# Selecting matmuls as 64x32 tiles on two banks, and GpSimd's products moved to VectorE, in an S5 and attention trunk

## The chip, the cores and the metric

The kernel runs on one core of a Trainium2 chip. The metric is the device time of one execution in microseconds (us); the time before is the median of three runs. One execution was also recorded by the hardware profiler. In its views PE is TensorE (matmuls), PEld its weight loads, DVE is VectorE, ACT is ScalarE, POOL is GpSimd, SP is SyncE, which issues the DMAs.

## The reference

The reference is a trunk of two layers on 256 tokens of 2048 channels, all in float32: an S5 state-space layer with a gated linear unit (GLU), a gated MLP with a short convolution, a latent attention layer, and a second such MLP. Each sub-layer is wrapped in two RMS norms.

```
x = x + rms(s5_mixer(rms(x)));   x = x + rms(conv_ffn_0(rms(x)))
x = x + rms(mla_mixer(rms(x)));  x = x + rms(conv_ffn_1(rms(x)))

def rmsnorm(x, g):
    y = x32 * lax.rsqrt(jnp.mean(x32 * x32, axis=-1, keepdims=True) + EPS) * g
def s5_mixer(u, ...):            # 128 groups of 16 channels, 64 complex states each
    x_re = jnp.einsum('blgp,gnp->blgn', ub, bb_re);  x_im = ...
    acc_re, acc_im, hl_re, hl_im = lax.associative_scan(combine, (a_r, a_i, x_re, x_im), axis=1)
    y = einsum(hs_re, c_re) - einsum(hs_im, c_im) + d_skip * ub
    val, gate = jnp.split(gelu(y) @ w_glu + b_glu, 2, axis=-1);  return val * sigmoid(gate)
def conv_ffn(h, ...):
    g = depthwise_conv(h @ w_gate) + conv_b;  return (gelu(g) * (h @ w_up)) @ w_down
```

## The kernel before

Every weight is streamed once from HBM in tiles of 1 MB (`raw`) and split in two parts, so that float32 accuracy comes out of reduced passes: ScalarE writes the high part (`whi`, L73), VectorE the rest (`wlo` = raw - whi, L74; with a gain folded in, L101). Where a weight tile is held back for later use, its parts are called x. Two or three matmuls then make one product (L108 to L110, L114 and L115). The token halves tb = 0, 1 hold 128 rows each.

The S5 layer is the stage from the start to about 262 us. It is computed as 16 blocks (nb = 16), eight groups of channels each. In a loop over the blocks the steps of three neighbouring blocks are written in between each other:

- `part_a`, the frames (L382 to L385) and the powers prepare tables of the recurrence: mostly VectorE (L430 to L435), some ScalarE (bc, L418 to L421).
- `part_k` makes the table K of the block: 128x32 matmuls (L399), one copy by ScalarE (L451) and an addition by VectorE (L452). Then the **selecting matmuls** (L466): their stationary operand is a column range of the constant tile cst that holds ones and zeros, their moving operand is K, so they only pick rows of K and put them elsewhere. There are two banks; into each go 2 x 2 x 4 matmuls: two strips j, an odd and an even part, and four column tiles b of 32 columns. The stationary operand is 128 rows by 32 columns, and in each all but 16 rows are zero. Behind each bank ScalarE copies it into TP (L471).
- `part_e` transposes (L479), `part_v` and `part_r` scan over the states (L495 to L506, matmul L511, then L513, L514), `part_h` makes H (L520), `part_c` the output (L399 with ET, TP, f and H).
- Once a quarter of the output is there, one step of the GLU (24 matmuls of 128x512, L108 to L110; sums L256, L258) stands in each block's place, from block 5 on.

After the S5 blocks `glu_rest` streams the rest of the GLU's weights; bias, sigmoid and product are L627 to L630.

Between the layers the row norms stand in TensorE's way. `finish_chunk` squares a chunk of 512 columns with sums (ScalarE, L139) and multiplies it by the norm's gain (L166): the last of four chunks on VectorE, the others on GpSimd. `rstd1` forms the inverse root: sum tot (L145), the power rs_y on GpSimd (L147), one Newton step on VectorE (L149 to L153). `post_norm` adds to the residual (L172, VectorE), squares, and multiplies by the next norm's gain (L178): the first two chunks on GpSimd, the others on VectorE. `pre_scale` writes the diagonal xh (L182), and the transposing matmuls L191 wait for it; all matmuls of the next layer stand behind these. Meanwhile the first weights of the next layer are split and held; in both FFNs two of these splits (slots 0 and 4 of `HOLD`) run on GpSimd, the others on VectorE.

Each engine works its own queue in order; the order in a queue is set when the kernel is built, by a scheduler that walks the program with buffers and priorities. So an edit in one place can shift the rows of a queue elsewhere.

Of the kernel before, what the change touches and what calls it, by code (L numbers as in the profile page):

```python
# [15 lines left out]
P = 128  # L16
D = 2048
S = 256
# [19 lines left out]
HOLD = ((0, 2), (4, 6), (8, None), (None, None))  # L38

C_ID, C_PS, C_PR, C_BO, C_DM, C_MK, C_CV = 0, 128, 256, 384, 512, 528, 592  # L40
C_SG, C_NSG, C_TPI, C_FR, C_RS, C_HP, C_MH, C_SL, C_END = 624, 625, 626, 627, 628, 629, 630, 638, 894


@with_exitstack
def tile_trunk(ctx: ExitStack, tc: tile.TileContext, a: dict):
# [4 lines left out]
    def T(pl, shape, dt=F32, tag=None, bufs=None):  # L50
        cnt[0] += 1
        kw = {"bufs": bufs} if bufs else {}
        return pl.tile(shape, dt, tag=tag, name=f"{tag}_{cnt[0]}", **kw)
# [11 lines left out]
    def accb():  # L65
        return T(ps, [P, 512], F32, "acc")
# [96 lines left out]
    def finish_chunk(f, fst, tb, n, g):  # L163
        c = f[tb][:, n * 512 : (n + 1) * 512]
        sq_acc(c, fst[tb][:, n : n + 1])
        (dve if n == NCH - 1 else pool).tensor_tensor(c, c, g[0][:, n * 512 : (n + 1) * 512], op=ALU.mult)  # L166

    def post_norm(f, fst, tb, x, xst, g):
        r = rstd1(fst[tb], D)
        for n in range(NCH):  # L170
            c = slice(n * 512, (n + 1) * 512)
            dve.scalar_tensor_tensor(x[tb][:, c], f[tb][:, c], r, x[tb][:, c], op0=ALU.mult, op1=ALU.add)  # L172
            if xst is None:
                sync.dma_start(a["out"][tb * P : (tb + 1) * P, c], x[tb][:, c])
                continue
            sq_acc(x[tb][:, c], xst[:, n : n + 1])
            if g is not None:
                (pool if n < 2 else dve).tensor_tensor(f[tb][:, c], x[tb][:, c], g[0][:, c], op=ALU.mult)  # L178

    def pre_scale(xst):  # L180
        d = T(env["ap"], [P, 512], F32, "xh", 2)[:, :P]
# [79 lines left out]
    def s5(f):  # L261
        with tc.tile_pool(name="s5", bufs=2) as q1:
# [175 lines left out]
            def part_k(sb, e1, ff):  # L438
# [17 lines left out]
                    op=ALU.add,  # L456
                )
                TP = T(q1, [P, 4, NG * P], F32, "TP")
                for jj in range(2):
                    bank = accb()  # L460
                    for j in range(2):
                        for odd in range(2):
                            o = C_SL + (2 * (2 * jj + j) + odd) * 32
                            for b in range(4):
                                r = 16 * (2 * b + odd)
                                pe.matmul(  # L466
                                    bank[32 * b : 32 * b + 32, j * 256 : (j + 1) * 256].rearrange("p (g c) -> p g c", g=NG),
                                    cst[:, o : o + 32], K[:, :, r : r + P],
                                    start=j == 0 and odd == 0, stop=j == 1 and odd == 1, tile_position=(0, 32 * b),
                                )  # L470
                    act.activation(TP[:, 2 * jj : 2 * jj + 2, :], bank.rearrange("p (j c) -> p j c", j=2), AF.Copy)  # L471
                return U, TP

            def part_e(e1):
# [207 lines left out]
    def ffn(l, tail, gains, f, fst, done):  # L682
        with tc.tile_pool(name=f"ff{l}", bufs=2) as q1:
# [42 lines left out]
            for part, npair in enumerate(PARTS):  # L726
                hid = []
                for pr in range(p0, p0 + npair):
                    banks = [wk(), wk()] if pr == 0 else [[wk(), wk()] for _ in range(2)]
                    held = []  # L730
                    for which, w in enumerate((wg, wu)):
                        for kh in range(2):
                            v = w[:, 8 * kh : 8 * kh + 8, pr * S : (pr + 1) * S]
                            if pr == 0:
                                held.append((which, kh, wunit(v, 8, S, slots=HOLD[len(held)], onpool=(0, 4))))
                            else:
                                inner(banks[which], kh, wunit(v, 8, S))
                    if held:
# [345 lines left out]
def _constants():  # L1084
# [20 lines left out]
    for j in range(4):  # L1105
        for odd in range(2):
            q = np.arange(16)
            c[32 * j + 16 + q, C_SL + (2 * j + odd) * 32 + 16 * odd + q] = 1.0
    return c


# [65 lines left out]
```

## Time and profile before

| what | us |
|---|---|
| median of three runs | 2207.73 (2205.02 to 2211.3) |
| the profiled execution's own time | 2209.45 |
| span of its profile | 2207.7 |
| S5, from the first select to the last block's work | 36.57 to 262 |
| busy in the span: TensorE, VectorE, ScalarE, GpSimd | 2109.7, 1415.1, 1125.0, 75.7 |
| waits of TensorE for xh at the three layer edges | 7.92, 8.42, 8.37 |
| selecting matmuls, busy in all | 60.3 |

A row of a group or timeline gives the start, the duration, the engine, the line and operation, output<-inputs, tile, shape and count; in square brackets stands how long the engine had been idle before, and what ended that. A float32 matmul appears as two passes where it is not split by hand, so a select block of 32 matmuls is 64 records.

### The profile page before, as it was taken

To read this page: it belongs to the slowest core of one execution; us is meant where nothing else is said; L and a number is where in the kernel's file an instruction comes from. 1 tells how busy PE (TensorE), PEld (TensorE's weight loads), DVE (VectorE), ACT (ScalarE), POOL (GpSimd) and SP (SyncE) were. 2 spreads that over 40 slices of the span, in tenths; PEclk is the share of its full clock that TensorE was granted. 3 is DMA by queue.
4 is the path that set the end of the run, shared out by engine and by line. 5 is a ranking of instruction groups with operands and counts; after the bars stand their busy time and mean duration, and the time that the engine had idled before them with its cause. 6 is when DMAs were issued, how large, how long until landed. Compare 5 with 4: busy or idle time off the path is not lost. (4 is left out here: it accounts for less than half of the span.)

```text
span 2207.7 us, 32426 instructions
## 1 busy us (share of the span) xinstructions
PE 2109.7 (96%) x13268; PEld 1779.4 (81%) x13268; DVE 1415.1 (64%) x1904; ACT 1125.0 (51%) x1695; POOL 75.7 (3%) x93
## 2 busy tenths in 40 slices
PE   3899999899999999999989999989999999999997
PEld 2666777888888888888878898788888888888886
DVE  7999675766456656655676665566646655665566
ACT  6676444455455435544464555545545544554444
POOL 0000010200000000000010000120000000000001
PEclk9999999999999999999999999999999999999999
DMA  4132376455555555556563434635555556555554
GB/s 129 47 100 75 103 246 208 148 191 189 183 195 184 190 191 190 186 178 201 185 200 121 145 122 137 212 128 179 186 191 191 191 178 203 189 188 181 197 184 149
DMA packets 280965, 374.80 MB, mean 170 GB/s; under 512 B 9200, under 2 KB 196208, under 8 KB 279792
## 3 DMA queue, kind: packets, MB, share of 16 engines
q1 hardware_dynamic: 280816, 372.73, 51.5%
q8 instruction: 104, 1.70, 0.3%
q14 instruction: 45, 0.37, 0.1%
HBM read 370.61 MB, written 2.10 MB: 169 GB/s over the span
## 5 line engine op out<-in xcount | busy, mean ns | idle before, releaser
L74 DVE TENSOR_TENSOR wlo<-raw,whi 128x1024 fp32r<-128x1024 f32 (+2 forms) x640 | 763.3, 1194 | 595.7 <-ACT whi L73 592.6
L73 ACT ACTIVATE whi<-raw 128x1024 fp32r<-128x1024 f32 (+2 forms) x640 | 658.3, 1031 | 646.8 <-PE wk L114 249.2
L114 PE MATMUL wk<-act,whi 128*128 128x512 f32 x2688 | 944.8, 396 | 0.0
L115 PE MATMUL wk<-act,wlo 128*128 128x256 f32 x2688 | 754.4, 281 | 0.0
L114 PEld LDWEIGHTS wk<-act,whi 128*128 128x128 f32 x2688 | 504.4, 188 | 121.1
L115 PEld LDWEIGHTS wk<-act,wlo 128*128 128x128 f32 x2688 | 507.8, 189 | 0.3
L109 PE MATMUL acc<-wlo,hh 128*128 128x512 f32 x652 | 255.8, 392 | 0.5
L108 PE MATMUL acc<-whi,hh 128*128 128x512 f32 x652 | 255.6, 392 | 0.0
L110 PE MATMUL acc<-whi,hl 128*128 128x512 f32 x652 | 254.3, 392 | 0.0
L109 PEld LDWEIGHTS acc<-wlo,hh 128*128 128x128 f32 x652 | 122.5, 188 | 28.4 <-DVE wlo L74 2.2
L108 PEld LDWEIGHTS acc<-whi,hh 128*128 128x128 f32 x652 | 122.5, 188 | 27.4 <-ACT hh L73 0.5
L110 PEld LDWEIGHTS acc<-whi,hl 128*128 128x128 f32 x652 | 122.5, 188 | 26.9
L108 PE MATMUL acc<-whi,act 128*128 128x512 f32 (+1 forms) x332 | 126.4, 381 | 0.9 <-ACT act L73 0.7
L109 PE MATMUL acc<-wlo,act 128*128 128x512 f32 (+1 forms) x332 | 124.8, 377 | 2.3 <-DVE wlo L74 2.3
L110 PE MATMUL acc<-whi,act 128*128 128x512 f32 (+1 forms) x332 | 124.2, 375 | 0.0
L166 POOL TENSOR_TENSOR f<-f,gb 128x512 f32<-128x512 f32 x24 | 37.3, 1555 | 1866.7 <-issue 1583.9
L763 DVE SCALAR_TENSOR_TENSOR cv<-gs,cw,cv 128x255 f32<-128x255 f32 (+1 forms) x168 | 77.2, 480 | 3.0
L109 PEld LDWEIGHTS acc<-wlo,act 128*128 128x128 f32 x332 | 62.5, 188 | 15.3 <-DVE wlo L74 4.4
L108 PEld LDWEIGHTS acc<-whi,act 128*128 128x128 f32 x332 | 62.5, 188 | 12.7 <-ACT act L73 1.0
L110 PEld LDWEIGHTS acc<-whi,act 128*128 128x128 f32 x332 | 62.5, 188 | 11.4 <-DVE act L74 0.4
L761 ACT ACTIVATE cv<-gs,cb,cw 128x256 f32<-128x256 f32 x84 | 50.5, 601 | 36.5 <-DVE gs L713 36.5
L466 PE MATMUL acc<-K,cst 128*32 128x256 f32 x1024 | 60.3, 388 | 5.0 <-DVE K L452 4.7
(285 smaller groups left out, 2409.3 us busy)
## 6 DMA issues: line engine op xcount, KB each, us to landing
raw<-in_w_gate SPq DMA_DIRECT2D x88, 1024.0 KB, 4.9
raw<-in_w_up SPq DMA_DIRECT2D x88, 1024.0 KB, 4.9
raw<-in_w_down SPq DMA_DIRECT2D x88, 1024.0 KB, 4.9
raw<-in_w_glu SPq DMA_DIRECT2D x32, 1024.0 KB, 6.1
raw<-in_w_o SPq DMA_DIRECT2D x16, 1024.0 KB, 5.0
raw<-in_w_ukv SPq DMA_DIRECT2D x8, 1024.0 KB, 5.4
gb<-in_norm_g SPq DMA_DIRECT2D x6, 1024.0 KB, 8.4
raw<-in_w_uq SPq DMA_DIRECT2D x8, 768.0 KB, 4.6
```

Of the source, the lines that this page charges most:

```text
L73: act.activation(hi, src, AF.Copy)
L74: (eng or dve).tensor_tensor(lo, src, hi.bitcast(F32), op=ALU.subtract)
L108: pe.matmul(o, lh, rh, start=first, stop=False)
L109: pe.matmul(o, lh, rl, start=False, stop=False)
L110: pe.matmul(o, ll, rh, start=False, stop=last)
L114: pe.matmul(ov, lh, r, start=first, stop=False)
L115: pe.matmul(ov[:, 0, :], ll, r[:, 0, :], start=False, stop=last)
L166: (dve if n == NCH - 1 else pool).tensor_tensor(c, c, g[0][:, n * 512 : (n + 1) * 512], op=ALU.mult)
L466: pe.matmul(bank[32 * b : 32 * b + 32, j * 256 : (j + 1) * 256].rearrange("p (g c) -> p g c", g=NG), cst[:, o : o + 32], K[:, :, r : r + P ...
L761: act.activation(cv[:, ft, :], gv[:, ft, :], AF.Identity, scale=cw[:, 2, n : n + 1], bias=cb[:, n : n + 1])
L763: dve.scalar_tensor_tensor(cv[:, ft, sh:], gv[:, ft, : S - sh], cw[:, 2 - sh, n : n + 1], cv[:, ft, sh:], op0=ALU.mult, op1=ALU.add,)
```

## The change

Two things change. First, the selecting matmuls: the stationary operand is now 64 rows by 32 columns. Row half jj = 0 reads rows 0 to 63 of K and writes bank 0, row half jj = 1 reads rows 64 to 127 and writes bank 1. Both banks are taken at the start, the innermost loop alternates between them, and the two copies into TP come behind all 32 matmuls. The constant tile becomes 128 columns narrower, since both halves use the same columns. Second, GpSimd gives up its share of the products L166 and L178 and of the weight splits L74; they go to VectorE. It keeps the powers (L147) and small memsets: 98 rows of its queue become 62, and VectorE's 1906 become 1942.

```diff
-C_SG, C_NSG, ..., C_SL, C_END = 624, 625, ..., 638, 894
+C_SG, C_NSG, ..., C_SL, C_END = 624, 625, ..., 638, 766
...
     def finish_chunk(f, fst, tb, n, g):
-        (dve if n == NCH - 1 else pool).tensor_tensor(c, c, g[0][:, n * 512 : (n + 1) * 512], op=ALU.mult)
+        dve.tensor_tensor(c, c, g[0][:, n * 512 : (n + 1) * 512], op=ALU.mult)
...
     def post_norm(f, fst, tb, x, xst, g):
-                (pool if n < 2 else dve).tensor_tensor(f[tb][:, c], x[tb][:, c], g[0][:, c], op=ALU.mult)
+                dve.tensor_tensor(f[tb][:, c], x[tb][:, c], g[0][:, c], op=ALU.mult)
...
+                banks = [accb() for _ in range(2)]
+                for j in range(2):
+                    for odd in range(2):
+                        for b in range(4):
+                            r = 16 * (2 * b + odd)
+                            for jj in range(2):
+                                o = C_SL + (2 * j + odd) * 32
+                                hp = slice(64 * jj, 64 * jj + 64)
+                                pe.matmul(
+                                    banks[jj][32 * b : 32 * b + 32, j * 256 : (j + 1) * 256].rearrange("p (g c) -> p g c", g=NG),
+                                    cst[hp, o : o + 32], K[hp, :, r : r + P],
+                                    start=j == 0 and odd == 0, stop=j == 1 and odd == 1, tile_position=(64 * jj, 32 * b),
+                                )
                 for jj in range(2):
-                    bank = accb()
-                    for j in range(2):
-                        for odd in range(2):
-                            o = C_SL + (2 * (2 * jj + j) + odd) * 32
-                            for b in range(4):
-                                r = 16 * (2 * b + odd)
-                                pe.matmul(
-                                    bank[32 * b : 32 * b + 32, j * 256 : (j + 1) * 256].rearrange("p (g c) -> p g c", g=NG),
-                                    cst[:, o : o + 32], K[:, :, r : r + P],
-                                    start=j == 0 and odd == 0, stop=j == 1 and odd == 1, tile_position=(0, 32 * b),
-                                )
-                    act.activation(TP[:, 2 * jj : 2 * jj + 2, :], bank.rearrange("p (j c) -> p j c", j=2), AF.Copy)
+                    act.activation(TP[:, 2 * jj : 2 * jj + 2, :], banks[jj].rearrange("p (j c) -> p j c", j=2), AF.Copy)
...
-                                held.append((which, kh, wunit(v, 8, S, slots=HOLD[len(held)], onpool=(0, 4))))
+                                held.append((which, kh, wunit(v, 8, S, slots=HOLD[len(held)])))
...
-            c[32 * j + 16 + q, C_SL + (2 * j + odd) * 32 + 16 * odd + q] = 1.0
+            c[32 * j + 16 + q, C_SL + (2 * (j % 2) + odd) * 32 + 16 * odd + q] = 1.0
```

Lines behind the select move by two in the changed kernel (L466 to L467, L471 to L473, L479 to L481, L495 to L497, L511 to L513); lines ahead of it keep their numbers. In the rows that follow, a number behind a name tells one use of a buffer from another.

TensorE's queue around the select of one early block, before:

```order
L479 MATMUL wk_450<-cst_73,e_86_350 128x128 x4
L479 MATMUL wk_456<-cst_73,e_86_350 128x128 x4
L466 MATMUL acc_413<-K_44_179,cst_73 32x256 x16
L466 MATMUL acc_431<-K_44_179,cst_73 32x256 x16
L511 MATMUL wk_462<-R_386,cst_73 128x256
```

And in the changed kernel (acc_413 and acc_414 are the two banks; the alternation goes on for 32 rows):

```order
L481 MATMUL wk_450<-cst_73,e_86_350 128x128 x4
L481 MATMUL wk_456<-cst_73,e_86_350 128x128 x2
L467 MATMUL acc_413<-K_44_179,cst_73 32x256
L467 MATMUL acc_414<-K_44_179,cst_73 32x256
...
L481 MATMUL wk_456<-cst_73,e_86_350 128x128 x2
L513 MATMUL wk_462<-R_386,cst_73 128x256
```

The two banks were filled one behind the other and are now filled in turns; two of the eight transposes of `part_e` moved behind the select here. From block 5 on the order of the other matmuls is as before.

VectorE's queue between FFN 0 and the attention, from the sum tot of the norm to the diagonal xh, before (x and raw are the attention's first weights, gkv the gain folded into them):

```order
L145 TENSOR_REDUCE tot_10186<-st_781_4240 128x1
L101 SCALAR_TENSOR_TENSOR x_1737_10374<-raw_10367,gkv_76,x_1737_10374 128x512
L149 TENSOR_SCALAR rs_m_1694_10190<-tot_10186 128x1
L101 SCALAR_TENSOR_TENSOR x_1737_10374<-raw_10367,gkv_76,x_1737_10374 128x512
L151 SCALAR_TENSOR_TENSOR rs_u_1695_10192<-rs_m_1694_10190,rs_y_1693_10188 128x1
L101 SCALAR_TENSOR_TENSOR x_1739_10393<-raw_10391,gkv_76,x_1739_10393 128x512
L153 SCALAR_TENSOR_TENSOR rs_r_1696_10194<-rs_u_1695_10192,rs_y_1693_10188 128x1
L101 SCALAR_TENSOR_TENSOR x_1739_10393<-raw_10391,gkv_76,x_1739_10393 128x512
L182 TENSOR_SCALAR xh_10184<-cst_73,rs_r_1696_10194 128x128
```

And in the changed kernel:

```order
L145 TENSOR_REDUCE tot_10186<-st_781_4240 128x1
L101 SCALAR_TENSOR_TENSOR x_1737_10374<-raw_10367,gkv_76,x_1737_10374 128x512
L149 TENSOR_SCALAR rs_m_1694_10190<-tot_10186 128x1
L101 SCALAR_TENSOR_TENSOR x_1737_10374<-raw_10367,gkv_76,x_1737_10374 128x512
L151 SCALAR_TENSOR_TENSOR rs_u_1695_10192<-rs_m_1694_10190,rs_y_1693_10188 128x1
L166 TENSOR_TENSOR f_4237<-f_4237,gb_4242 128x512
L153 SCALAR_TENSOR_TENSOR rs_r_1696_10194<-rs_u_1695_10192,rs_y_1693_10188 128x1
L166 TENSOR_TENSOR f_4237<-f_4237,gb_4242 128x512
L182 TENSOR_SCALAR xh_10184<-cst_73,rs_r_1696_10194 128x128
```

Two products L166 of the other token half, which stood in GpSimd's queue, are now ahead of xh, and two weight splits L101 have gone behind it.

VectorE's queue between the attention and FFN 1, from the residual's sum to xh, before:

```order
L172 SCALAR_TENSOR_TENSOR x_3285<-f_10326,rs_r_2141_12753,x_3285 128x512 x4
L178 TENSOR_TENSOR f_10326<-x_3285,gb_10333 128x512 x2
L74 TENSOR_TENSOR x_2186_12932<-raw_12927,x_2186_12932 128x1024
L74 TENSOR_TENSOR x_2188_12937<-raw_12935,x_2188_12937 128x1024
L145 TENSOR_REDUCE tot_12773<-st_1724_10330 128x1
L149 TENSOR_SCALAR rs_m_2149_12777<-tot_12773 128x1
L151 SCALAR_TENSOR_TENSOR rs_u_2150_12779<-rs_m_2149_12777,rs_y_2148_12775 128x1
L153 SCALAR_TENSOR_TENSOR rs_r_2151_12781<-rs_u_2150_12779,rs_y_2148_12775 128x1
L182 TENSOR_SCALAR xh_12771<-cst_73,rs_r_2151_12781 128x128
```

And in the changed kernel, from the second pair of chunks on (L172 x2 and L178 x2 stand ahead of it):

```order
L172 SCALAR_TENSOR_TENSOR x_3285<-f_10326,rs_r_2141_12753,x_3285 128x512 x2
L178 TENSOR_TENSOR f_10326<-x_3285,gb_10333 128x512 x2
L74 TENSOR_TENSOR x_2185_12929<-raw_12927,x_2185_12929 128x1024
L74 TENSOR_TENSOR x_2186_12932<-raw_12927,x_2186_12932 128x1024
L145 TENSOR_REDUCE tot_12773<-st_1724_10330 128x1
L74 TENSOR_TENSOR x_2188_12937<-raw_12935,x_2188_12937 128x1024
L149 TENSOR_SCALAR rs_m_2149_12777<-tot_12773 128x1
L166 TENSOR_TENSOR f_10327<-f_10327,gb_10332 128x512
L151 SCALAR_TENSOR_TENSOR rs_u_2150_12779<-rs_m_2149_12777,rs_y_2148_12775 128x1
L145 TENSOR_REDUCE tot_12865<-st_1723_10329 128x1
L74 TENSOR_TENSOR wlo_12941<-raw_12935,whi_12940 128x1024
...
L182 TENSOR_SCALAR xh_12771<-cst_73,rs_r_2151_12781 128x128
```

Ahead of xh stand now two more L178, the split x_2185 that GpSimd had, one L166 and one split wlo. On the GLU's edge to FFN 0 the same exchange takes place: two splits, two L178 and one L166 more ahead of xh.

More of the change, by code (lines that the diff above doesn't have):

```diff
@@ L40 @@
 C_ID, C_PS, C_PR, C_BO, C_DM, C_MK, C_CV = 0, 128, 256, 384, 512, 528, 592
-C_SG, C_NSG, C_TPI, C_FR, C_RS, C_HP, C_MH, C_SL, C_END = 624, 625, 626, 627, 628, 629, 630, 638, 894
+C_SG, C_NSG, C_TPI, C_FR, C_RS, C_HP, C_MH, C_SL, C_END = 624, 625, 626, 627, 628, 629, 630, 638, 766
 @with_exitstack
```

## The prediction

> **What bounds the kernel now.** I read the page's head first, then the busy times of each stretch, then what the engines wait for in the stretches that the change touches.
>
> ```profile
> span 2207.7 us, 32426 instructions
> PE 2109.7 (96%) x13268; PEld 1779.4 (81%) x13268; DVE 1415.1 (64%) x1904; ACT 1125.0 (51%) x1695; POOL 75.7 (3%) x93
> ```
>
> TensorE is busy for 96% of the span, so at first sight every microsecond taken from it counts. That is an average over stages. The change takes TensorE work out of one stage only, the S5 layer, which ends near 262 us. The next view cuts that stage at the start of the first select, of block 6, of block 13, and at the end of the S5 work. The columns are the stretch, its length, busy time of each engine (instructions), granted clock, DMA share, GB/s.
>
> ```profile
> core 0: us, PE busy (x) PEld busy (x) DVE busy (x) ACT busy (x) POOL busy (x), PEclk, DMA share, GB/s
> 36.57:113.14 76.57, 64.32 (x1039) 43.90 (x1038) 71.49 (x120) 48.58 (x104) 0.40 (x5) 0.93 0.23 68
> 113.14:218.75 105.61, 98.17 (x1384) 71.74 (x1385) 96.60 (x148) 75.06 (x139) 0.00 (x0) 1.00 0.29 85
> 218.75:262.00 43.25, 42.86 (x568) 31.38 (x568) 26.10 (x45) 21.59 (x38) 0.00 (x0) 1.00 0.17 51
> ```
>
> Three regimes stand there. In blocks 0 to 5 VectorE has 76.57 - 71.49 = 5.08 us without work and TensorE 12.25: VectorE is the bound. In blocks 6 to 12 VectorE has 9.01 spare and TensorE 7.44: the two are nearly level. In blocks 13 to 15 TensorE has 0.39 spare and VectorE 17.15: TensorE is the bound. So a microsecond off TensorE is worth a whole one in the last three blocks, and elsewhere only what VectorE's own waits can give.
>
> **The select.** One select block, its first moments, and the weight loads of the same moments:
>
> ```profile
> 129.33 3.66 PE L466 MATMUL acc<-K,cst 128*32 128x256 f32 x64 [0.52 <-DVE K L452]
> 129.33 0.42 PE L466 MATMUL acc<-K,cst 128*32 128x256 f32 x4 [0.52 <-DVE K L452]
> 129.33 0.16 PEld L466 LDWEIGHTS acc<-K,cst 128*32 128x32 f32 x8 [0.75 <-DVE K L452]
> L466 PEld LDWEIGHTS acc<-K,cst x1024: 106/110/178, 36.6 to 246.6; 128*32 128x32 f32 x171
> L466 PE MATMUL acc<-K,cst x1024: 379/379/634, 36.6 to 246.8; 128*32 128x256 f32 x171
> ```
>
> The 32 matmuls of a block appear as 64 passes (1024 over 16 blocks), and four start together at 129.33, one for each column tile. That makes 16 rounds; one pass lasts 0.379, so a round follows the other after (3.66 - 0.379) / 15 = 0.219 us. Afterwards the same 64 passes of 256 columns run on half the rows, and two row halves may run at once: eight to a round, eight rounds, 7 x 0.219 + 0.379 = **1.91 us, 1.75 less per block**. If the halves do not overlap it stays at 3.66. If the weights are also exposed, it is 16 x (0.219 + 0.110) = 5.3. No row of this trace shows 64-row tiles, so these are the two bounds. I take 1.91, because the four column tiles, the nearest row, do start together, and the halves write to two banks.
>
> On the weight loads: the second row of the three shows eight loads beginning within 0.16 us while the four passes of the row above it, on all 128 rows, run for 0.42. The Trainium skill, "TensorE: Matmul & The Clock Gate", Part 3 (the mechanism), says that a weight load overlaps matmuls in flight only when its row group differs; by that the select before would be 5.3 us, an estimate, and it measures 3.66. The trace does not agree, so the rule gets only the small chance of rival 4.
>
> **Blocks 13 to 15** (TensorE bound): 3 x 1.75 = -5.2 us. VectorE's 17.15 spare covers it.
>
> **Blocks 6 to 12** (7 x 1.75 = 12.25 us off TensorE, VectorE with 9.01 spare). What matters is which of VectorE's waits end in TensorE. These are its waits there that do:
>
> ```profile
> 138.87 1.23 DVE L74 TENSOR_TENSOR wlo<-raw,whi 128x1024 fp32r<-128x1024 f32 x1 [0.80 <-ACT whi L73]
> 140.71 1.23 DVE L74 TENSOR_TENSOR wlo<-raw,whi 128x1024 fp32r<-128x1024 f32 x1 [0.61 <-ACT whi L73]
> ...
> 192.09 1.23 DVE L434 TENSOR_TENSOR e<-z,bc 128x1024 f32<-128x1024 f32 x1 [0.59 <-ACT bc L419]
> 195.07 0.69 DVE L258 TENSOR_TENSOR f<-acc,f 128x512 f32<-128x512 f32 x1 [0.96 <-PE acc L110]
> 197.52 1.23 DVE L74 TENSOR_TENSOR wlo<-raw,whi 128x1024 fp32r<-128x1024 f32 x1 [1.76 <-ACT whi L73]
> 212.10 1.22 DVE L74 TENSOR_TENSOR wlo<-raw,whi 128x1024 fp32r<-128x1024 f32 x1 [0.38 <-ACT whi L73]
> ```
>
> Those on ScalarE hang on TensorE too, since ScalarE itself waits for matmuls there:
>
> ```profile
> 137.78 1.06 ACT L73 ACTIVATE whi<-raw 128x1024 fp32r<-128x1024 f32 x1 [0.76 <-PE acc L110]
> 196.43 1.06 ACT L73 ACTIVATE whi<-raw 128x1024 fp32r<-128x1024 f32 x1 [3.88 <-PE acc L110]
> ```
>
> No block can give more than the 1.75 by which TensorE gets ahead: 0.80 + 0.61, then 0.59, then 1.75 of the 2.72 at 195 to 197, then 0.38, together 4.1. Bounds 0 and -9.01; I take **-4**, and count VectorE's other waits there at nothing, because no late matmul stands ahead of them.
>
> **Blocks 0 to 5**: bounds 0 and -5.08. VectorE is 93% busy here (71.49 of 76.57) and TensorE has 12.25 spare, so work taken from TensorE mostly adds to its pauses. I take **-1**, nearer to nothing. Sum for S5: -5.2 - 4 - 1 = **-10.2**. The order of TensorE barely changes else. ScalarE's copy of the first bank now stands behind all passes instead of after half of them; half of 3.66 is 1.83 and the whole is now 1.91, so the first bank is no later and the second 1.7 earlier.
>
> **GpSimd to VectorE.** A finishing product (L166) costs GpSimd 1.71 and VectorE 0.69. More telling is that a two-input VectorE operation grows when it meets one of GpSimd's:
>
> ```profile
> 305.82 1.71 POOL L166 TENSOR_TENSOR f<-f,gb 128x512 f32<-128x512 f32 x1 [8.63 <-ACT junk L139]
> 306.30 1.78 DVE L627 TENSOR_TENSOR sg<-f,bias 128x512 f32<-128x512 f32 x1
> ...
> 309.75 0.80 PE L108 MATMUL wk<-whi,act 128*128 128x512 f32 x1 [1.87 <-ACT whi L73]
> ...
> 401.15 0.68 DVE L627 TENSOR_TENSOR sg<-acc,bias 128x512 f32<-128x512 f32 x1
> ...
> 2190.09 0.69 DVE L166 TENSOR_TENSOR f<-f,gb 128x512 f32<-128x512 f32 x1 [0.17 <-ACT junk L139]
> ```
>
> L627 takes 1.78 at 306.30 and 0.68 at 401.15, where GpSimd is quiet; ScalarE's sg waits for it, and TensorE waits 1.87 for the cast behind sg. In the rest of the GLU this is worth **-1** (0 to -1.87): 1.1 back from the collision, while the products that VectorE takes over lie behind TensorE's matmuls.
>
> Between the layers TensorE stands still until VectorE has written xh, so VectorE's queue is the path. The three edges and the tail:
>
> ```profile
> 392.61 2.34 DVE L151 SCALAR_TENSOR_TENSOR rs_u<-rs_m,rs_y 128x1 f32<-128x1 f32 x1 [0.47 <-POOL rs_y L147]
> 395.18 4.78 DVE L172 SCALAR_TENSOR_TENSOR x<-f,rs_r,x 128x512 f32<-128x512 f32 x4
> 399.88 1.28 DVE L178 TENSOR_TENSOR f<-x,gb 128x512 f32<-128x512 f32 x2
> 405.30 0.55 PE L191 MATMUL acc<-xh,f 128*128 128x128 f32 x1 [7.92 <-DVE xh L182]
> ...
> 1154.95 0.16 DVE L145 TENSOR_REDUCE tot<-st 128x1 f32<-128x5 f32 x1
> 1156.28 4.23 POOL L166 TENSOR_TENSOR f<-f,gb 128x512 f32<-128x512 f32 x3
> 1157.56 1.83 DVE L101 SCALAR_TENSOR_TENSOR x<-raw,gkv,x 128x512 fp32r<-128x512 f32 x1
> 1160.45 0.74 DVE L101 SCALAR_TENSOR_TENSOR x<-raw,gkv,x 128x512 fp32r<-128x512 f32 x1
> 1161.11 0.27 DVE L182 TENSOR_SCALAR xh<-cst,rs_r 128x128 f32<-128x128 f32 x1
> ...
> 1418.68 3.03 DVE L74 TENSOR_TENSOR x<-raw,x 128x1024 fp32r<-128x1024 f32 x2 [0.33 <-ACT x L73]
> 1434.75 4.82 DVE L172 SCALAR_TENSOR_TENSOR x<-f,rs_r,x 128x512 f32<-128x512 f32 x4
> 1439.49 3.43 DVE L178 TENSOR_TENSOR f<-x,gb 128x512 f32<-128x512 f32 x2
> 1446.36 0.29 DVE L182 TENSOR_SCALAR xh<-cst,rs_r 128x128 f32<-128x128 f32 x1
> ...
> 2194.25 2.74 DVE L172 SCALAR_TENSOR_TENSOR x<-f,rs_r,x 128x512 f32<-128x512 f32 x4
> 2199.20 1.10 DVE L166 TENSOR_TENSOR f<-f,gb 128x512 f32<-128x512 f32 x1 [1.00 <-ACT junk L139]
> ```
>
> - GLU to FFN 0: L172 falls from 4.78 to 2.74, as at 2194.25, and L151, on one column like tot, from 2.34 to about 0.16: -4.2. In their place VectorE has two weight splits of 1.22, two L178 of 0.64 and one L166 of 0.69 ahead of L182: +4.4. **0** (from -1 to +1).
> - FFN 0 to attention: from tot at 1154.95 to the end of xh it takes 6.43. Afterwards, by the queue, tot and three more on one column 0.64, two L101 of 0.74, two L166 of 0.69 and L182 0.27: 3.8, and I add 0.7 for waits on ScalarE's squares, 4.5. **-1.9** (0 to -2.6).
> - Attention to FFN 1: from 1434.75 to the end of xh 11.90. Afterwards L172 2.74, four L178 2.56, three splits 3.66, one more split 1.22 and an L166 0.69 that slip in, six on one column 0.96 and L182 0.29: 12.1, less some 1.1, because neighbours overlap by about 0.08 (L172 at 1434.75 ends at 1439.57, and the next starts at 1439.49). -0.9, and -0.5 for the two splits at 1418.68, 3.03 where two alone are 2.44: **-1.4** (+0.5 to -2.5).
> - Tail: L166 at 2199.20 falls from 1.10 to 0.69, and its start hangs on ScalarE: **-0.5** with the product that GpSimd runs beside it (0 to -1).
>
> Edges: -3.8. The steady weight streams of FFN and attention keep their order, and I cost them at nothing; the few L166 that VectorE takes over there hide behind TensorE's matmuls.
>
> **Sum.** -10.2 - 1 - 3.8 = -15.0, against the profiled execution's own 2209.45 us (its span 2207.7 and 1.75 around it): 2194.45, so **2194.5**. That execution is 1.7 above the median of 2207.73, well inside the runs' own spread.
>
> **Rivals.**
> 1. The row halves do not run at once; the select stays at 3.66 and only the GLU and the edges give: -4.8, 2204.6. For it: no 64-row tile is in this trace. Against it: four tiles start together, so the array does run tiles side by side. Chance 0.12.
> 2. VectorE gives back everything before 218 us, since it is 91 to 93% busy there; a lower clock after longer pauses of TensorE (0.93 in blocks 0 to 5) works the same way. What is left is -5.2 - 4.8: 2199.5. Chance 0.20.
> 3. All of VectorE's waits go: -5.1 - 9.0 - 5.2 - 4.8 = -24.1, 2185. For it: the two engines feed each other, so one delay can stand behind several waits. Against it: ScalarE and VectorE wait for one another too. Chance 0.10.
> 4. Slower: halves that neither overlap nor hide their weights, so that a select costs 5.3, 1.6 more. Blocks 13 to 15 pay 4.9; blocks 6 to 12 would pay 11.3 and have 7.44 to cover it, so 4 to 11, say 7.5; less 4.8 elsewhere: +7.6, 2217. It turns from gain to loss at a select of about 4.9 us, where 3 x 1.2 and 7 x 1.2 - 7.44 reach 4.8. Chance 0.08, since the loads are hidden today.
>
> By the Trainium skill, "TensorEngine Tiling (Array Packing)", Key Properties, a change of tiling mode drains TensorE, which speaks against mixing modes. Here 128x32 and 128x128 alternate already, and L511 starts at 132.92 in the row
>
> ```profile
> 132.92 0.70 PE L511 MATMUL wk<-R,cst 128*128 128x256 f32 x2
> ```
>
> while the select ends at 132.99: the trace shows no drain worth a term.
>
> **How the numbers follow.** The forecast has 0.50. What can be told from no change is about 0.3%, 6.6 us: below 2201 is faster, above 2214 slower. The forecast, rival 3 and most of rival 2 are faster, 0.74; rival 1 and the rest of rival 2 are the same, 0.18; rival 4 is slower, 0.08. The range runs from rival 3's 2184 to 2207, a little above rival 1; what it leaves out is rival 4 and the far side of rival 3.
>
> **What would show it.** Right: select blocks of about 1.9 us, eight passes starting together; TensorE in blocks 13 to 15 shorter by 5; S5 ending near 252; L172 at 2.74 at every edge; TensorE's long waits for xh shorter by 0, 1.9 and 0.9. Wrong: a select above 3 us, blocks 6 to 12 as long as before, or new waits of TensorE in the GLU that return what S5 gained.

## The result and the profile after

The changed kernel takes 2191.82 us in the median of four runs (2187.58 to 2193.81), the one before 2207.28 beside it: a ratio of 0.9925, with a 95% interval of 0.9911 to 0.9938, that is 15.5 us less. When both ran again later, side by side, the ratio was 0.994 (0.9925 to 0.9955), 12.2 us less. The forecast was 2194.5. The profiled execution of the changed kernel took 2187.58 (span 2185.8), which is the fastest of its four runs, so differences between the two profiles come out larger than those between the medians.

The head of the page, as before, shows TensorE 30.7 us and GpSimd 56 us less busy:

```profile
span 2185.8 us, 32404 instructions
PE 2079.0 (95%) x13268; PEld 1764.2 (81%) x13268; DVE 1408.8 (64%) x1940; ACT 1122.4 (51%) x1695; POOL 19.8 (1%) x57
```

VectorE has 36 instructions more and 6 us less to do, so what it took over adds less than it got back elsewhere. The select, one block and its first moments in TensorE's timeline:

```profile
127.39 1.96 PE L467 MATMUL acc<-K,cst 64*32 64x256 f32 x64 [0.26 <-DVE K L452]
127.39 0.45 PE L467 MATMUL acc<-K,cst 64*32 64x256 f32 x8 [0.26 <-DVE K L452]
```

Eight passes start together where it was four, and a block takes 1.96 us instead of 3.66 (1.91 was forecast). The three stretches of the S5 layer, cut at the same selects as before and, at the end, at the same place of the last block's work:

```profile
36.43:111.32 74.89, 54.96 (x1039) 39.22 (x1038) 70.75 (x119) 47.41 (x106) 0.43 (x6) 0.93 0.22 65
111.32:213.04 101.72, 87.00 (x1384) 66.12 (x1384) 96.37 (x149) 74.57 (x137) 0.00 (x0) 1.00 0.31 91
213.04:251.50 38.46, 37.71 (x568) 28.94 (x568) 25.89 (x44) 21.36 (x39) 0.00 (x0) 1.00 0.20 57
```

They are 1.68, 3.89 and 4.79 us shorter (forecast 1, 4 and 5.2). In the first two, TensorE lost some 9 to 11 us of work and its idle time grew: 19.9 us in the first (12.25 before), 14.7 in the second (7.44).

The edges between the layers, in the timelines of VectorE and TensorE:

```profile
383.44 1.41 DVE L172 SCALAR_TENSOR_TENSOR x<-f,rs_r,x 128x512 f32<-128x512 f32 x2
393.24 0.58 PE L191 MATMUL acc<-xh,f 128*128 128x128 f32 x1 [7.29 <-DVE xh L182]
...
1141.96 0.15 DVE L145 TENSOR_REDUCE tot<-st 128x1 f32<-128x5 f32 x1
1142.75 0.74 DVE L101 SCALAR_TENSOR_TENSOR x<-raw,gkv,x 128x512 fp32r<-128x512 f32 x1
1145.34 1.01 PE L191 MATMUL acc<-xh,x 128*128 128x128 f32 x3 [5.92 <-DVE xh L182]
...
1428.87 5.61 PE L191 MATMUL acc<-xh,f 128*128 128x128 f32 x32 [7.41 <-DVE xh L182]
```

Two L172 take 1.41 where four took 4.78, no L101 takes 1.83, and TensorE waits 0.6, 2.5 and 1.0 us less for xh (forecast 0, 1.9 and 0.9).

### The profile page after: what moved, and what is told of

It reads as the page before. It is cut to its first block, busy times and chain, and to the rows that moved or that the text cites. A ratio compares the mean times of both kernels' runs of the same rounds, so it can differ in the third digit from the quotient of the medians.

```text
span 2185.8 us, 32404 instructions
## 1 busy us (share of the span) xinstructions
PE 2079.0 (95%) x13268; PEld 1764.2 (81%) x13268; DVE 1408.8 (64%) x1940; ACT 1122.4 (51%) x1695; POOL 19.8 (1%) x57
## 4 chain that ended last, share of the span: by engine, by line
PE 82%; DVE 10%; DMA 4%; ACT 3%; issue 1%; POOL 0%; SPq 0%; DVEq 0%; POOLq 0%; ACTq 0%
PE wk L114 29%; PE wk L115 15%; PE acc L108 9%; PE acc L109 9%; PE acc L110 9%; DMA raw<-in_w_glu 3%; PE wk L108 2%; PE wk L109 2%; PE wk L110 2%; DVE wlo L74 2%; PE acc L191 1%; DVE x L74 1%; ACT whi L73 1%; DVE f L431 1%; DVE f L430 1%
## 5 line engine op out<-in xcount | busy, mean ns | idle before, releaser
L74 DVE TENSOR_TENSOR wlo<-raw,whi 128x1024 fp32r<-128x1024 f32 (+2 forms) x640 | 761.0, 1191 | 584.0 <-ACT whi L73 579.3
L114 PE MATMUL wk<-act,whi 128*128 128x512 f32 x2688 | 941.9, 395 | 0.0
L114 PEld LDWEIGHTS wk<-act,whi 128*128 128x128 f32 x2688 | 504.1, 188 | 119.3
L714 ACT ACTIVATE us<-wk 128x256 f32<-128x256 f32 x84 | 31.7, 380 | 60.3 <-PE wk L115 60.3
L714 ACT ACTIVATE gs<-wk 128x256 f32<-128x256 f32 x84 | 32.0, 381 | 59.8 <-PE wk L115 59.8
```

Source lines behind the costliest of these rows:

```text
L74: (eng or dve).tensor_tensor(lo, src, hi.bitcast(F32), op=ALU.subtract)
L114: pe.matmul(ov, lh, r, start=first, stop=False)
L714: act.activation(z[:, ft, :], two[ft][:, S:], AF.Copy)
```

## Experiments

The stages below are differences of starts in TensorE's timeline: S5 from the first select's start to the last's; the rest of the GLU from there to the last matmul ahead of the wait for xh, less that select's own time; then the three waits. FFN 0 runs from the end of the first wait to the start of the second, FFN 1 from the end of the third to TensorE's last matmul, and the tail from there to the end. "Half clock" is the time in S5 at a granted clock of 0.5, which comes in pieces of 3.4 us or multiples of it.

| profiled kernel | S5 | half clock in it | rest of the GLU | waits for xh | FFN 0, FFN 1 | tail |
|---|---|---|---|---|---|---|
| before | 206.9 | 10.2 | 150.2 | 7.92, 8.42, 8.37 | 747.7, 749.8 | 11.1 |
| changed | 198.3 | 10.2 | 149.3 | 7.29, 5.92, 7.41 | 746.2, 746.6 | 10.3 |
| changed, again | 202.2 | 20.5 | 153.0 | 7.29, 7.07, 7.04 | 745.6, 747.2 | 10.3 |
| select alone | 200.5 | 23.9 | 155.7 | 8.19, 7.42, 8.88 | 748.4, 748.3 | 11.1 |
| select alone, again | 203.4 | 27.3 | 153.0 | 8.37, 8.47, 8.70 | 746.8, 748.7 | 11.1 |
| GpSimd alone | 205.7 | 6.8 | 151.8 | 7.23, 7.42, 7.04 | 746.3, 747.1 | 10.3 |
| products L166 back on GpSimd | 198.7 | 13.7 | 152.8 | 7.11, 8.43, 6.82 | 746.8, 747.5 | 11.1 |
| splits L74 back on GpSimd | 202.9 | 20.5 | 155.8 | 8.14, 6.01, 10.20 | 748.3, 746.6 | 10.3 |

### The two parts apart

The select alone keeps GpSimd's three choices of before; GpSimd alone keeps the select of before.

```diff
 e1_select_only, against the changed kernel
+        (dve if n == NCH - 1 else pool).tensor_tensor(c, c, g[0]...)
+                (pool if n < 2 else dve).tensor_tensor(f[tb][:, c], ...)
+        ... wunit(v, 8, S, slots=HOLD[len(held)], onpool=(0, 4))
 e2_gpsimd_only, against the kernel before: the same three lines the other way
```

> The select of the changed kernel, with GpSimd's products and splits where they were before. If the two parts of the change are independent and the select's length is what S5 gained: select blocks of 1.96 us, the last select starting near 234.7 us (before 243.5), the GLU's matmuls ending near 387 (before 397.4), and TensorE's waits for xh as before, 7.9, 8.4 and 8.4. Time about 2207.3 - 10.4 = 2197. Rival: part of the S5 gain came with GpSimd's move; then the last select starts later than 236.

> The select as before, GpSimd's products and splits on VectorE as in the changed kernel. If independent: the last select starts at 243.5 as before, the GLU's matmuls end near 396.4, the waits for xh are 7.3, 5.9 and 7.4, the tail 0.8 shorter. Time about 2207.3 - 5 = 2202. Rival: the move costs VectorE in the weight streams what the edges give; then no difference, 2207.

The select alone gave 0.9979 (0.9966 to 0.9993), 2203.2 us, only 4 less; GpSimd alone 0.9966 (0.9955 to 0.9978), 2199.6 us, 7.7 less. The last select of the first began at 236.9, past the 236 that the rival had named, though GpSimd has next to nothing to do in S5. So the select seemed to be worth less than half of the forecast, and GpSimd more than half as much again.

> The select alone once more. In its first profile one weight tile of the GLU landed 11.1 us after its issue (7.5 in the kernel before and in the changed one), TensorE waited 2.4 us for it and then ran at half clock, and the rest of the GLU took 157.7 us against 153.9 before. If that was chance: 151 to 154 us in this profile, TensorE's waits for xh near 8, and a time near 2198. Rival: without GpSimd's move the earlier end of S5 always runs into late weights; then again 156 to 158, and 2203.

> The changed kernel once more, for the spread of its stages: if the stages are stable, from the last select to the end of the GLU's matmuls 151 to 153 us, the waits for xh 7.2, 5.9 and 7.2 to 7.4, and the ratio to before within 0.991 to 0.994. Rival: the first profile was a lucky one; then the GLU takes 155 or more, and the ratio is above 0.995.

Both were run again, side by side. The select alone now gave 0.9963 (0.9949 to 0.9976); its GLU took 155.0 us from the last select's start, between the theory's 154 and the rival's 156. The changed kernel gave 0.994, inside the 0.991 to 0.994 of the theory only at its edge, with the 155 us in the GLU that the rival named (TensorE waited 1.9 us there for a cast whose weight tile came late, and 3.4 us at half clock followed). Averaged, the select is worth about 0.3% (the mean of 0.9979 and 0.9963 is 0.9971, 6.4 us), GpSimd's part about 0.34%; their product 0.9937 is what the whole gives. The parts are independent within the error, but the error is large: side by side the changed kernel was only 4.2 us below the select alone (2197.4 and 2201.6), where GpSimd alone had given 7.7.

What differs between two executions of one program stands in the granted clock. The same stretch of the changed kernel's two profiles; in the first, a pause of TensorE in its timeline

```profile
89.28 0.33 PE L497 MATMUL wk<-cst,vs 128*128 128x128 f32 x1 [2.71 <-ACT vs L488]
```

and two stretches behind it (the granted clock stands behind POOL's share):

```profile
87.00:95.00 8.00, 4.96 (x104) 4.00 (x112) 8.00 (x14) 4.42 (x12) 0.00 (x0) 1.00 0.01 4
101.00:109.00 8.00, 6.71 (x34) 5.17 (x38) 7.79 (x14) 7.97 (x19) 0.25 (x4) 1.00 0.12 36
```

In the second, the same pause

```profile
89.13 0.33 PE L497 MATMUL wk<-cst,vs 128*128 128x128 f32 x1 [2.68 <-ACT vs L488]
```

and the same stretches:

```profile
87.00:95.00 8.00, 5.82 (x87) 4.92 (x88) 7.17 (x13) 3.71 (x11) 0.00 (x0) 0.79 0.01 2
101.00:109.00 8.00, 5.95 (x18) 4.45 (x19) 7.80 (x13) 6.56 (x15) 0.25 (x4) 0.79 0.05 14
```

The pause of TensorE is the same, 2.7 us; behind it the clock stayed at 1.00 once and fell to half for 3.4 us the other time (0.79 over 8 us). The second stretch lies behind another such pause, 2.71 us up to 102.24 in the first profile and 2.70 up to 102.99 in the second.

What each piece of half clock costs can be followed from select to select. In block 4 the second profile is 0.12 us ahead of the first (83.06 against 83.18), in block 5 it is 0.76 behind, in blocks 6 to 8 it is 2.08 behind and in block 9 3.45. Between these steps the lag changes by less than 0.2 us up to block 14. The steps of 0.9, 1.3 and 1.4 us lie where the second profile alone has a piece of half clock, at 90.6, 104.2 and 155.4. They make up 3.6 of the 3.9 us by which its S5 is longer.

In the kernel before, TensorE's longest pause from 70 to 113 us is 1.67 us. A piece of half clock follows that one too, at 84.2, with TensorE busy for 1.70 of the 3.41 us ahead of it. So half clock is not new with the short select, and no run here shows from which pause on it comes.

Over the eight profiles with the new select and GpSimd in any of these settings (the six in the table, and two below that leave S5's queues alone: 199.6 with 10.2, 202.8 with 20.5), a straight line gives 0.26 us more of S5 for each us at half clock, with a correlation of 0.82. That is a correlation over chance, not an intervention; the pair above, one program with equal pauses, is the closest to one.

### The row halves one behind the other

The nested loops are shortened to one line here.

```diff
-                for j in range(2): for odd in range(2): for b in range(4): for jj in range(2): ...
+                for jj in range(2): for j in range(2): for odd in range(2): for b in range(4): ...
```

> As the changed kernel, but all 16 matmuls of row half 0 are issued before the 16 of row half 1, as two banks one behind the other; the tiles are still 64x32. If the halves must be issued in turns to run at once: rounds of four passes, select blocks of 3.6 to 3.7 us, the last select near 243, time about 2202. Rival: TensorE looks far enough ahead in its queue to start the other half, or the shorter tiles alone do it: blocks near 2 us, time 2192.

It gave 0.9962 (0.9951 to 0.9973), 2197.5 us, and neither of the two lengths:

```profile
127.67 2.85 PE L467 MATMUL acc<-K,cst 64*32 64x256 f32 x64 [0.54 <-DVE K L452]
127.67 0.42 PE L467 MATMUL acc<-K,cst 64*32 64x256 f32 x4 [0.54 <-DVE K L452]
```

In the records of that block four rounds of four passes start alone, at 0, 0.24, 0.46 and 0.67 us; from 0.91 on a second stream of four runs beside the first, 0.01 to 0.05 behind it. The records do not name the half; but four passes fill the four column tiles of one, so the second stream has to be half 1. Then half 0 starts its last round at 1.54 and half 1 at 2.45. So the halves run together as soon as TensorE reaches the second one, while 12 of the first one's 32 passes still wait: it looks ahead, but not past all of the 32. Issuing them in turns is worth 2.85 - 1.96 = 0.89 us per block, and the 64-row tiles issued half by half the other 0.81. S5 took 202.1 us (13.7 at half clock), between 206.9 and 198.3; from block 13 to block 15 it is 1.7 us shorter than before, twice 0.81, as the bound there demands.

### The select twice

```diff
+                for _ in range(2):
                     for j in range(2): ...
```

> As the changed kernel, but the 32 matmuls of a select are issued twice with the same result, so that its length is about that of before (3.7 us) and all else stays. If the S5 gain is the select's length alone: the last select near 243.5 as before, time about 2202. Rival: part of it came from the altered order of the first blocks, or from both copies behind the matmuls: the last select starts earlier than 241.

It took 2222.3 us, 1.0076 (1.0057 to 1.0095), slower than the kernel before although a select takes 3.69 us like the old one. The last select began at 263.9, 20 us after that of before. It doesn't test the theory: with the select's rows doubled the scheduler ordered VectorE's queue in S5 otherwise, and the loss lies in blocks 0 to 12 (8.5 and 10.9 us), where VectorE has little to spare; 10 us more at half clock are in it. From block 13 to block 15, where the order matters least, it took 25.8 against 24.7 before. One select there took 4.68 us, 1.0 more than the others, with a halt of 0.75 between its passes at a granted clock of 1.00, for which the profile names no cause. Without that one the length alone would decide there. For an early block the run says nothing.

### Sixteen passes at once

```diff
+                banks = [accb() for _ in range(4)]
+                for odd in range(2): for b in range(4): for j in range(4):
+                    pe.matmul(banks[j][32 * b : 32 * b + 32, :256]..., cst[32 * j : 32 * j + 32, o : o + 32], ..., tile_position=(32 * j, 32 * b))
+                for j in range(4):
+                    act.activation(TP[:, j, :], banks[j][:, :256], AF.Copy)
```

> As the changed kernel, but with tiles of 32 rows by 32 columns: each of the four strips of K has its own row tile and its own bank, 16 matmuls in place of 32, and four copies into TP. If sixteen passes run at once: four rounds or fewer per bank pair, 32 passes in two rounds, 0.219 + 0.38 = 0.6 us per select in place of 1.96; in blocks 13 to 15, where TensorE is the bound, 1.3 us less per block, in the others a third of it: S5 about 7 us shorter at the same granted clock, time about 2188. Rivals: the four banks are also the GLU's, so that TensorE waits for TP's copies, and S5 is no shorter; or the longer pauses bring more half clock, and the gain goes there.

The expectation counted wrongly: there are still 32 matmuls, so sixteen at once would make four rounds and 1.04 us. (The loops are shortened to one line above.) It gave 0.9973 (0.996 to 0.9986), 2203.9 us, slower than the changed kernel. The select did get shorter:

```profile
128.54 1.50 PE L466 MATMUL acc<-K,cst 32*32 32x256 f32 x64 [0.54 <-DVE K L452]
```

From block 13 to block 15 it saved 0.97 us, about what 2 x 0.46 makes. But blocks 6 to 12 took 111.0 us instead of 101.7, and TensorE's waits there name the first rival, the GLU's matmuls that want a bank which still holds TP:

```profile
PE acc L108 <- ACT TP L472: 6.1, 3, 2.4
```

The second rival has a share as well: 6.8 us of that stretch were at half clock, none in the changed kernel's first profile, and S5 as a whole had 30.7. The order of VectorE's queue changed here too, so the 6.1 us of waits are shown, and how the 9 divide is not settled.

### Which of GpSimd's jobs matters

The first run below has only the first of the three lines of the select alone, for L166, the second only the last, for the splits.

> As the changed kernel, but the products L166 of the first three chunks are GpSimd's again. If they are what cost the edge between FFN 0 and attention: TensorE waits 7.4 to 8.4 there (5.9 in the changed kernel), the tail is 0.8 longer, the waits of the other two edges stay at 7.2 to 7.4; the GLU about 1 longer; time about 2191.8 + 4 = 2196. Rival: the queue's new order makes the gain, not the place of the products; then the wait stays near 6.

> As the changed kernel, but the two weight splits L74 of each FFN (slots 0 and 4) are GpSimd's again; the products stay on VectorE. If the splits' collisions matter at the edges of the FFNs: L151 at 2.3 us again beside a split on GpSimd, TensorE's waits for xh near 7.9 ahead of FFN 0 and 7.5 to 8 ahead of FFN 1 (7.2 and 7.0 to 7.4 in the changed kernel), the wait ahead of the attention unchanged at 5.9 to 7.1. Time about 1 us above the changed kernel. Rival: GpSimd takes 4.9 us of work off VectorE at each edge, so both waits are shorter, 6.5 or less.

With the products L166 back on GpSimd the kernel took 2197.3 us (0.9954, 0.9939 to 0.9969), which the times do not tell from the changed kernel beside it (2197.4). The stages do: the wait ahead of the attention is 8.43 again and the tail 11.1. Over all profiles that wait is 7.42 to 8.47 with L166 on GpSimd and 5.87 to 7.42 with it on VectorE. The collision of before is back row by row:

```profile
1147.00 4.29 POOL L166 TENSOR_TENSOR f<-f,gb 128x512 f32<-128x512 f32 x3
1147.19 1.22 DVE L151 SCALAR_TENSOR_TENSOR rs_u<-rs_m,rs_y 128x1 f32<-128x1 f32 x1
1148.33 1.83 DVE L101 SCALAR_TENSOR_TENSOR x<-raw,gkv,x 128x512 fp32r<-128x512 f32 x1
1150.09 1.22 DVE L153 SCALAR_TENSOR_TENSOR rs_r<-rs_u,rs_y 128x1 f32<-128x1 f32 x1
```

With the splits back on GpSimd (2198.0 us; 0.9951, 0.9929 to 0.9973) the waits ahead of the FFNs grow to 8.14 and 10.2, the latter beyond what the theory allowed. GpSimd's split falls on VectorE's one-column L151:

```profile
1433.44 2.41 DVE L151 SCALAR_TENSOR_TENSOR rs_u<-rs_m,rs_y 128x1 f32<-128x1 f32 x1 [0.53 <-POOL st L143]
1433.44 2.38 POOL L74 TENSOR_TENSOR x<-raw,x 128x1024 fp32r<-128x1024 f32 x1
1443.70 1.60 POOL L147 TENSOR_TENSOR rs_y<-tot,cst 128x1 f32<-128x1 f32 x1 [7.88 <-DVE tot L145]
```

In the last row it is the other way round: the power on GpSimd takes 1.60 instead of 0.54, beside a split of 1.22 on VectorE. The rest of the GLU was 155.8, but a late weight tile is in it, so nothing is read from that.

### GpSimd's reads by themselves

In S5 GpSimd has no work, so the collision can be bought there alone. Once it reads, once it only writes; both keep the order of VectorE's queue.

```diff
 e7_pool_reads
+                for _ in range(4):
+                    pj = T(q1, [P, NG, P], F32, "pj", 1)
+                    pool.tensor_tensor(pj, U, U, op=ALU.mult)
 e7b_pool_writes
+                pool.tensor_tensor(pj[:, :, :1], U[:, :, :1], U[:, :, :1], op=ALU.mult)
+                for _ in range(6):
+                    pool.memset(pj, 0.0)
```

> As the changed kernel, but in each S5 block GpSimd also multiplies U by itself four times into a buffer that nobody reads; the queues of the other engines are as in the changed kernel. GpSimd is otherwise without work there. If GpSimd's reads hold up VectorE's two-input operations, as at the edges: some operations of 0.4 to 1.3 us (L430 to L435, L498 to L500) grow by up to a GpSimd operation's length, and S5 gets longer by 10 us or more, to a last select at 245 or later (234.7 and 238.4 in the two profiles of the changed kernel). Rival: each engine reads by itself; S5 stays within its spread.

> The control of the run with GpSimd's reads: as the changed kernel, but in each S5 block GpSimd waits for U with one small product of two columns and then only fills the same buffer with zeros, six times, without reading. If it is GpSimd's reading that holds VectorE's operations with two SBUF operands (0.687 to 0.946 us for the scan R, 0.420 to 0.633 for the sum w, 0.419 to 0.605 for the product w<-R,co in that run): they stay at 0.69, 0.42 and 0.42, and the last select starts between 234 and 239. Rival: any work on GpSimd holds them; then they grow as there, and the last select is at 245 or later.

With reads, one execution took 2211.8 us and the last select began at 251.6. Groups of VectorE's instructions in S5 (busy, mean ns, idle before), in the changed kernel:

```profile
L508 DVE TENSOR_TENSOR_SCAN R<-dc,w 128x256 f32<-128x256 f32 x15 | 10.3, 687 | 0.0
L502 DVE TENSOR_TENSOR w<-w,w 128x256 f32<-128x256 f32 x15 | 6.3, 420 | 0.0
L500 DVE TENSOR_TENSOR w<-wk,co 128x256 f32<-128x256 f32 x15 | 6.3, 418 | 3.6 <-PE wk L498 3.5
```

with GpSimd's reads:

```profile
L511 DVE TENSOR_TENSOR_SCAN R<-dc,w 128x256 f32<-128x256 f32 x15 | 14.4, 958 | 0.0
L505 DVE TENSOR_TENSOR w<-w,w 128x256 f32<-128x256 f32 x15 | 9.1, 605 | 0.0
L503 DVE TENSOR_TENSOR w<-wk,co 128x256 f32<-128x256 f32 x15 | 6.2, 416 | 2.4 <-PE wk L501 2.3
```

and with its writes:

```profile
L513 DVE TENSOR_TENSOR_SCAN R<-dc,w 128x256 f32<-128x256 f32 x15 | 10.3, 687 | 0.0
L507 DVE TENSOR_TENSOR w<-w,w 128x256 f32<-128x256 f32 x15 | 6.3, 421 | 0.0
L505 DVE TENSOR_TENSOR w<-wk,co 128x256 f32<-128x256 f32 x15 | 6.3, 420 | 4.0 <-PE wk L503 3.9
```

The scan R and the sum w, with two operands in SBUF, grow by some 40% on average; the product that takes one operand from a PSUM bank (wk) does not, and none of the three grows when GpSimd only writes. The growth is that of the operations which meet one of GpSimd's: with reads, the 12 scans that overlap one take 1.03 us and the 3 others 0.68. With the writes 9 scans overlap a fill and take 0.69. GpSimd is busy for 56 us in S5 with the reads and for 36 with the control. The longer products L430 to L435 do the same, 1.48 to 1.63 us beside a read and 1.21 to 1.35 without, but fewer of them meet one, so that their means grow by 5 to 8% only. S5 took 213.6 us with the reads, of which 34.1 were at half clock, so its length is not the collision's alone. With writes the time was 2194.9 and the last select at 239.2, just beyond the 239 named, with 20.5 us at half clock. The Trainium skill, "SBUF — State Buffer", section "SBUF: two separate sides", says that VectorE and GpSimd share one pair of ports by an exclusive lock, which a two-operand VectorE operation needs only against a GpSimd operation that reads; these three profiles agree.

### Loads of x later

> As the changed kernel, but the two 1 MB loads of x for the residual stand two GLU weights later in SyncE's program, after the second gain's load. If those loads share the DMA engines with weights that TensorE waits for, between 262 and 282 us: the rest of the GLU is 1 to 3 us shorter, near 149, time about 2190. Rival: the gain's 1 MB, which now comes where x was, costs as much; no difference within 1 us.

Here the two loads of x are issued later in the program. The scheduler put them only three and five places later in SyncE's queue and the next gain's 1 MB, of the same size, into their places, so the GLU's weights had as much beside them: 154.0 us from the last select's start to the GLU's end, between the 151.2 and 155.0 of the changed kernel's two profiles. The ratio was 0.9923 (0.9905 to 0.9941), not to be told from the changed kernel's 0.994 beside it. It says nothing on the question and is no shown improvement.

## Why the prediction was right, point by point

**The total** was right, 2194.5 against 2191.8 and 2197.4 in the two measurements, and so was the sign. Its two large terms, however, were off in opposite directions, and that they cancelled is luck.

**The select's length** was right: eight passes at a time, 1.96 us against 1.91. The two bounds were 1.91 and 5.3; the rival that weights would be exposed, and the one that the halves would not overlap, are both refuted by the same row. That the order in turns is what brings the lower end, and not the tile's shape alone, was not in the prediction: out of turn it is 2.85.

**S5's gain of 10.2 was an upper value.** The first profile shows 8.6 up to the last select's start and 1.7 for that select itself, 10.3. But over the eight profiles with the new select S5 took 201.1 us on average against 206.3 in the two with the old one: 5.2 and 1.7, 6.9 us, and the two runs of the select alone gave 6.4. The mis-sized steps are the terms for blocks 0 to 12, "I take -4" and "I take -1". By the same averages blocks 6 to 12 are 2.9 us shorter, and blocks 0 to 5 are 0.6 longer, with single profiles from 74.9 to 78.2 against 75.4 and 76.6. From block 13 to block 15, with two selects and so 3.4 us less work for TensorE, 3.0 to 3.1 came back in seven of the eight profiles and 2.6 in one: nearly a whole microsecond for each one taken, as forecast.

The reading behind "I take -4" was right. Of VectorE's waits that the prediction summed, 5.1 us as they stand there, 1.8 are left in the changed kernel (0.47 ahead of e, 1.29 ahead of wlo), and the four others are gone in both of its profiles. The longest that it set aside, 1.65 ahead of the wlo at 154.36, is still 1.64.

What takes the gain back is the clock, as far as the runs show: with 10.2 us at half clock, as before, S5 took 198.3 and 199.6, near the forecast; with 20 to 27 us it took 202.4 on average, 3.4 more. This mechanism stood in the prediction, as the second half of rival 2 and with no price of its own; the term came out about a third smaller on average. One rival was left untested: up to about 170 us VectorE's rows also stand in another order in the changed kernel (behind that they are the same), and no run parts this from the select's length.

**GpSimd's part was probably too small**: 4.8 forecast, about 7.5 measured alone (4.9 to 9.9 by the interval), though only 4.2 lay between the select alone and the changed kernel side by side. The edges: from the three profiles with all of GpSimd's old work to the changed kernel's two and that of GpSimd alone, the mean waits fall from 8.16, 8.10 and 8.65 to 7.27, 6.80 and 7.16, so 0.9, 1.3 and 1.5, and the tail by 0.8: 4.5, against 3.8 for the same four terms (0.5 of it a collision ahead of the third wait). The first was forecast at 0 and gave 0.9; "at nothing" also failed for the FFNs. They are shorter by 1.6 and 2.0 in the same comparison. A part of the second goes with the clock behind the shorter wait: the 32 transposes that follow xh took 6.75 us before and 5.61 after, at a granted clock of 0.69 and 0.81 over the 10 us from their start. Where the remainder comes from is open: in long stretches L114 takes 0.399 or 0.391 us at a granted clock of 1.00, as from 700 to 760 us in the kernel before

```profile
L114 PE MATMUL wk<-act,whi 128*128 128x512 f32 x144 | 50.9, 399 | 0.0
```

and in the changed one:

```profile
L114 PE MATMUL wk<-act,whi 128*128 128x512 f32 x107 | 37.1, 391 | 0.0
```

No run here intervened on that, and it does not follow GpSimd's work alone: the select alone has 0.399 there in one profile (FFN 0 748.4) and 0.391 in the other (746.8).

**The rest of the GLU**, forecast at -1, is not shown either way. The wait that the term named did fall, from 1.87 to 0.86, and it is 1.9 in the four profiles in which L166 is GpSimd's and 0.9 in seven others. But other waits grew there: TensorE's waits for wlo from 250 to 330 us sum to 2.7 before and 5.9 with GpSimd alone, and to 3.3 on average in those four against 4.9 in the seven. That VectorE's own L166 delays these splits is the likely reason and was not isolated. And this stage varies more than the term from run to run: it took 149.3 to 155.8 us, the most where a weight tile came late and half clock followed, with the DMA engines 84% busy from 250 to 290 us in the changed kernel. So the prediction's "the products that VectorE takes over lie behind TensorE's matmuls" is not borne out here.

**The rivals.** That VectorE gives everything back ahead of block 13 (0.20) is refuted for blocks 6 to 12, which were shorter in all eight profiles with the new select; but ahead of block 13 only 2.3 us of the forecast 5 came out on average, about midway between the forecast and this rival. That all of VectorE's waits go (0.10) is refuted: 5.35 of its 9.01 us of spare time in blocks 6 to 12 is still there. The slower case needed a select of 4.9 us or more.

## What to carry to other kernels

A microsecond taken from an engine is worth a microsecond only where that engine is the bound; elsewhere much of it becomes a pause, and here a pause of 2.7 us was in one execution followed by 3.4 us at half clock, and each such piece cost 0.9 to 1.4 us. Where a matmul can do with half the rows, issue the two halves in turns and into two banks (1.96 us against 2.85 one behind the other), and look at who else uses those banks before going to four. GpSimd is no free second VectorE: a product moved to it holds up the VectorE operations with two operands in SBUF that run beside it, so it belongs where VectorE has none on the path.

## What the runs showed of the hardware that was not expected

- Matmuls of the other row half overtake those ahead of them in the queue: with half 0's 32 passes issued first, half 1 started 0.91 us into the block, when 12 of half 0's passes had not started.
- The same pause of 2.7 us was followed by half clock in one execution and not in another of the same program whose timeline was 0.15 us apart. Half clock came in pieces of 3.4 us, and three of them set the S5 layer back by 0.9, 1.3 and 1.4 us. In the kernel before one followed a pause of 1.67 us.
- The collision goes both ways: beside VectorE's split the power on GpSimd took 1.60 us instead of 0.54.
- A few more rows in TensorE's queue can change the order that the scheduler gives VectorE's: with the doubled select, as long as the old one, S5 took 20 us more than before. How much of that is the order was not isolated.
